# Strassen's algorithm for the fourth column block of w1 and w3 in an fp32 decoder trunk

## The chip, the core and the metric

The kernel runs on one core of a Trainium2 chip. A core has five engines that run their own instruction streams and meet at semaphores: TensorE (PE, matrix products into PSUM), VectorE (DVE), ScalarE (ACT), GpSimd (POOL) and SyncE (SP, which here only issues transfers), and 16 DMA engines that move data between HBM and the on-chip SBUF. The metric is the device time of one execution in microseconds, lower is better; the profile of one further execution shows where the time lies.

## The reference

Two layers, each of three sublayers with a layer norm behind it: an FFN, a mixer, an FFN. 256 tokens, width 1024, FFN width 2816, everything in float32.

```python
def _swiglu(x, w1, w3, w2):
    return (jax.nn.silu(x @ w1) * (x @ w3)) @ w2
...
    for l in range(DEPTH):
        h = _swiglu(x, ffn_w1[l, 0], ffn_w3[l, 0], ffn_w2[l, 0])
        x = _layernorm(ALPHA * x + 0.5 * h, ln_g[l, 0], ln_b[l, 0])
        h = _mixer(x, l, w_in[l], gate_b[l], ...)
        x = _layernorm(ALPHA * x + h, ln_g[l, 1], ln_b[l, 1])
        h = _swiglu(x, ffn_w1[l, 1], ffn_w3[l, 1], ffn_w2[l, 1])
        x = _layernorm(ALPHA * x + 0.5 * h, ln_g[l, 2], ln_b[l, 2])
```

The change concerns the four FFNs: x (256 x 1024) times w1 and w3 (1024 x 2816), silu of the first times the second, and its transpose h as the left side of the product with w2 (2816 x 1024).

## The kernel before

Every number is kept as a high part (fp32r, made by ScalarE: `A.activation(hi, src, AF.Copy)`) and a low part (what is left, made by VectorE's subtraction), and each product is three matmuls: high x high, high x low, low x high (`three`, line 259). One matmul has 128 rows of tokens (an x tile as the stationary operand) and 512 columns of weights; the contraction runs over 8 tiles of 128.

Weights come as pieces of 128 x 2048 floats (1 MB, four k-tiles of 512 columns). `fetch` (line 152) issues the transfer on SyncE's queue into one of four `raw` buffers; `stream` (line 165) splits it into two pairs of high and low tiles of 128 x 1024 out of eight `hi` and eight `lo` buffers, in steps of `sub` columns. SyncE, ScalarE and VectorE run ahead of TensorE as far as these buffers allow. A tile's buffer is free when its last reader is done; who wants it stands at the head of its queue until then.

An FFN (`ffn`, line 710) takes the first 16 and the last 4 of the 22 column tiles as five blocks of 512 columns (`NB = 5`), and the two tiles left, 16 and 17, with the weights as the stationary operand (`gemm_a2`, line 264). The first block of the first FFN goes through `gemm_first` (line 451). The others go through `gemm_b2` (line 423): four transfers (w1 and w3, each in two halves of k); first all of them for the upper 128 tokens, then all for the lower 128, so that all eight pairs of high and low tiles of the block are held until the second pass frees them. At the end of each pass `done` (line 718) applies silu on ScalarE (723), multiplies on VectorE (724) and hands the 128 x 512 result to `turned` (730). This brings it into transposed form beside the following matmuls: GpSimd parts the floats into two planes of 16-bit halves (`parted`, 196), a transposing DMA on SyncE's queue turns them (`moved`, 201), GpSimd joins them again (`joined`, 206), and h is split into high and low parts (743, 745).

The order on TensorE is the program's order. The work beside it is written as generators: `beside` (line 137) registers one, and `beat` (124), called after each group of matmuls, counts time in beats of 12 matmuls of 512 columns and resumes the generators that are due. So `wait` in `turned` is the number of beats between `parted` and the transposing DMA. The other engines' instructions are put into their queues by a scheduler that follows the program's order (`tc.cur_priority`, raised by `step` with each fetch) where buffers allow; `behind(ins)` puts an instruction behind another one on the same engine.

The product with w2 (`gemm_seven`, line 323) already uses Strassen's algorithm for the first eight k-tiles: with 2 x 2 blocks of h (two halves of tokens, two of k) and of w2, seven block products in place of eight, of sums of blocks. The sums of h are made by `sums_of_h` (752). Sums of weight blocks are made by `plus` (VectorE) or by `gather` (a transfer on GpSimd's queue that adds to what is in the buffer). Between the products the other k-tiles run (`between`, 386).

The norm behind each FFN (`Norm`, 543) loads scale and shift into the pair of `bc` buffers of the pool `res` (`bc_load`, 537). The tiles of `done` use the same `bc` buffers for odd blocks (the second and the fourth), and the `val` buffers for even ones. In the last FFN ScalarE scales the loaded row at once (559).

PSUM has eight banks of 128 x 512 floats, four with the tag `main`, four with `side`. SBUF tiles of 128 x 512 floats come from the pools `tmp` (`main`: 3, `side`: 4) and `act` (`slot`: 26).

Of the kernel before, what the change touches and what calls it, by code (L numbers as in the profile page):

```python
# [54 lines left out]
def trunk(ctx, tc, x, xT, w13a, w13b, w2, wb, wqk, wu, wg, wgr, wbr, wbrr, wo, gateb, gatebr, sgug, sgub, sguwT, sgubias, lam, diffg,  # L55
# [96 lines left out]
    def fetch(src, width=CH, raw=None):  # L152

        step()
        if raw is None:
            raw = raw_pool.tile([P, CH], F32, tag="raw", name=name("raw"))
        for g in gate:
            g[0] -= 1
        while len(gate) > 1 and gate[1][0] < 0:
            gate.pop(0)  # L160
        with behind(gate[0][1] if gate and gate[0][0] < 0 else None):
            loaded[0] = nc.sync.dma_start(raw[:, :width], src).ins
        return raw
# [32 lines left out]
    def parted(src, out):  # L196

        for w in range(2):
            G.tensor_copy(out=planes(out)[:, w], in_=numbers(src)[:, w])  # L199
# [10 lines left out]
    def transposed(src, out, via, lead, first, second, eng, to=None):  # L210

        if lead:
            yield lead
        with behind(behind_norm[0] if lead else None):
            parted(src, out)
        yield first
        with behind(loaded[0]):
            moved(out, via)  # L220
        yield second
        joined(via, out if to is None else to, eng)
# [99 lines left out]

    def gemm_seven(src, xh, xl, sums, spare, ln, done):
# [13 lines left out]
        def gather(raw, more):  # L337
            step()
            for o in range(0, CH, HC):
                G.dma_start(raw[:, o : o + HC], more[:, o : o + HC], accum_op=ALU.add)  # L340
            return raw

        def plus(raw, more):
            for o in range(0, CH, HC):
                V.tensor_tensor(out=raw[:, o : o + HC], in0=raw[:, o : o + HC], in1=more[:, o : o + HC], op=ALU.add)  # L345
            return raw

        def pieces(raw):
            out = []
            for o in range(0, CH, HC):  # L350
                hi = hi_pool.tile([P, HC], F32R, tag="hi", name=name("whi"))
                lo = lo_pool.tile([P, HC], F32R, tag="lo", name=name("wlo"))
                split(hi, lo, raw[:, o : o + HC])
                out.append((hi, lo))
            return out

        def product(ps, x, w, start, stop):
            for k in range(4):
                hi, lo = (v[:, k % 2 * 512 : k % 2 * 512 + 512] for v in w[k // 2])
                for n, (y, o) in enumerate(((hi, 0), (lo, 0), (hi, 1))):  # L360
                    PE.matmul(ps, x[o](k), y, start=start and k == n == 0, stop=stop and k == 3 and n == 2,  # L361
                              skip_group_check=True)
                beat(0.25)

# [6 lines left out]
        def rows(t, c, k0, piece, o=0, n=512):  # L371
            for j in range(2):
                k = k0 + j
                hi, lo = (w[:, j * 512 + o : j * 512 + o + n] for w in piece)
                for m, (y, x) in enumerate(((hi, xh), (lo, xh), (hi, xl))):
                    PE.matmul(q[c][t][:, :n] if o == 0 else more[:, :n], x(k)[:, t * P : (t + 1) * P], y,  # L376
                              start=k == 8 and m == 0 and (c, t) != (1, 0), stop=k == FT - 1 and m == 2, skip_group_check=True)
            beat(n / 1024)

        def block(t, k0):  # L380
            return tuple(lambda k, f=f: f(k0 + k)[:, t * P : (t + 1) * P] for f in (xh, xl))
# [161 lines left out]
    class Norm:  # L543
# [6 lines left out]
        def __init__(self, l, i, scale, eps, after, last=False):  # L550
            self.scale, self.eps, self.last, self.done, self.front = scale, eps, last, set(), i
            self.ends, self.xhi, self.xlo = [None] * NT, {}, {}
# [122 lines left out]
        def affine(self, t, h, src, xf, pieces, two=None):  # L675
            self.done.add((t, h))
            k = 0
# [32 lines left out]
    def ffn(l, f, i, norm, last=False):  # L710
        xh, xl = parts(both)
        h_hi = [act.tile([P, 512], F32R, tag="slot", name=name("hhi")) for _ in range(FT // 2)]
        h_lo = [act.tile([P, 512], F32R, tag="slot", name=name("hlo")) for _ in range(FT // 2)]
        hh, hl = view(h_hi), view(h_lo)

        def front(n, wait):

            def done(t, ps):
                pool, tag = ((act, "val"), (res, "bc"))[n % 2]
                p = pool.tile([P, D], F32, tag=tag, name=name("planes"), bufs=2).rearrange("p (w c) -> p w c", w=2)  # L720
                s = p[:, 1]
                with behind(norm.xhi[1, 0] if norm and (n, t) == (0, 0) else None):
                    silu[0] = A.activation(s, ps[0], AF.Silu).ins  # L723
                added[0] = V.tensor_tensor(out=s, in0=s, in1=ps[1], op=ALU.mult).ins  # L724
                beside(turned(n, t, s, p, wait[t]), 0)
                if norm is None and (n, t) == (1, 0):
                    beside(setup(s[:, :1]), 0)
            return done

        def turned(n, t, s, p, wait):  # L730
            lead = 3.5 if n == 0 and norm else 0
            to = slots("held", 2)[0] if n < 2 else p[:, 0]
            yield from transposed(s, p[:, 0], p[:, 1], lead, wait - lead, 0.6, G, to)
            x = to.rearrange("p (k t) -> p k t", k=4)
# [3 lines left out]
            for j in range(2) if (n, t) != (0, 1) else ():  # L738
                k = (n * 4 if n < NB - 1 else FT - 4) // 2 + j
                hi, lo = (v[k].rearrange("p (k t) -> p k t", k=2)[:, :, t * P : (t + 1) * P] for v in (h_hi, h_lo))  # L740
                f = x[:, 2 * j : 2 * j + 2]
                with behind(silu[0]):
                    A.activation(hi, f, AF.Copy)
                with behind(added[0]):
                    V.tensor_tensor(out=lo, in0=f, in1=hi.bitcast(F32), op=ALU.subtract)
# [6 lines left out]
        def sums_of_h():  # L752

            h11, h21, h12, h22 = (held[v] for v in ((0, 0), (0, 1), (1, 0), (1, 1)))
            made = [[[v[j].rearrange("p (k t) -> p k t", k=2)[:, :, P:] for j in range(2)] for v in (h_hi, h_lo)]]
            made += [[slots("sum", 2, F32R) for _ in range(2)] for _ in range(2)]
            made.append([[tmp.tile([P, 512], F32R, tag="side", name=name("sum"), bufs=4)] for _ in range(2)])
            sums[:] = [tuple(lambda k, v=v: hh_(v, k) for v in (h_hi, h_lo))]
            sums.extend(tuple(lambda k, v=v: v[0][:, k * P : (k + 1) * P] for v in m) for m in made[1:])
            for n, (out, a, b, op) in ((0, (h22, h21, h22, ALU.subtract)), (2, (h21, h11, h21, ALU.subtract)),  # L760
                                       (1, (h11, h22, h11, ALU.subtract)), (3, (h12, h12, h11, ALU.add))):
                V.tensor_tensor(out=out, in0=a, in1=b, op=op)
                w = 512 // len(made[n][0])
                for j, (hi, lo) in enumerate(zip(*made[n])):
                    f = out[:, j * w : (j + 1) * w]
                    split(hi, lo, f.rearrange("p (k t) -> p k t", k=2) if n == 0 else f)
                yield 1

        def hh_(v, k):
            return v[k // 2][:, k % 2 * T + P : k % 2 * T + T]  # L770

        for n in range(NB):
            srcs = [w13b[l, f, m * NB + n] for m in range(2)]
            if n == 0 and norm is None:
                gemm_first(srcs, front(n, (10.3, 10.3)))
            else:
                gemm_b2(srcs, xh, xl, front(n, (13.3, 10.3)), norm=norm if n == 0 else None)
        for j in range(FA, FT - 4, 2):
            for m, z in gemm_a2([w13a[l, f, j - FA + m] for m in range(2)], both, lambda m: t512("silu")):
# [3 lines left out]
                split(hh(j + m), hl(j + m), s)  # L783
# [400 lines left out]
```

## Time and profile before

| | us |
|---|---|
| median of three runs | 1199.59 (1199.42 to 1200.43) |
| the profiled execution, device time | 1198.81 |
| its span, first to last instruction | 1197.1 |
| mean granted TensorE clock | 0.999 of full speed |

| stretch of the profiled execution | us from the start |
|---|---|
| first FFN: blocks, tiles 16 and 17, w2 | 5.1 to 183.1 |
| first layer's mixer, second FFN | 183.1 to 597.4 |
| third FFN: five blocks | 597.4 to 706.2 |
| third FFN: tiles 16 and 17 | 706.2 to 717.3 |
| third FFN: w2 | 717.3 to 775.0 |
| second layer's mixer, fourth FFN, end | 775.0 to 1197.1 |

How to read it: engines run beside each other, so busy times do not add up to the span. A row of a group reads line, engine, operation, output and inputs by the program's names, shapes, count, then busy us and mean ns of one, then the idle time of the engine before them and what ended it. A row of windows gives, for a stretch in us, the busy time and instruction count of each engine, the granted clock, the share of the DMA engines and GB/s. A row of the chain of waits in order of time has start, duration and the work. A row of waits has engine, line, what was waited for, the total us, how often, the longest. A row of transfers has the queue, the count, the size and the median us from issue to landing. Matmuls are pipelined: the duration of one (about 390 ns) is longer than the spacing of two.

### The profile page before, as it was taken

The numbers are of one execution on the slowest core, as the hardware profiler recorded it, in microseconds if no ns is written. First come the engines' busy times: TensorE is split into PE (matmuls) and PEld (weight loads), VectorE is DVE, ScalarE is ACT, GpSimd is POOL, SyncE is SP. The second block draws the span as 40 slices with busy tenths as digits, with TensorE's granted clock in tenths as the row PEclk, the third lists the DMA queues.
The fourth block names the chain that finished last, engine by engine and source line by source line (L and its number), as shares of the span: only waits on it lengthen the run. The fifth ranks groups of instructions, "written<-read, shape, count | busy, mean of one in ns | idle before, by whom it ended". The sixth has DMA issues, their size and how long they took to land.

```text
span 1197.1 us, 16880 instructions
## 1 busy us (share of the span) xinstructions
PE 1191.1 (100%) x5819; PEld 1002.1 (84%) x5819; DVE 958.4 (80%) x1632; ACT 745.9 (62%) x1424; POOL 363.0 (30%) x458
## 2 busy tenths in 40 slices
PE   9999999999999999999999999999999999999998
PEld 8888888888888888888888888888888888888887
DVE  6677989797689985769886769888966989777795
ACT  7466667668855664646665656666788556564670
POOL 1425201256421233251042351004564012325310
PEclk9999999999999999999999999999999999999999
DMA  9957966767865667689676679586666764775880
GB/s 350 332 163 238 273 263 211 260 198 233 243 218 169 211 220 220 193 245 265 238 241 205 196 241 275 223 287 232 214 203 200 254 193 150 269 230 178 265 253 36
DMA packets 126310, 271.97 MB, mean 227 GB/s; under 512 B 88672, under 2 KB 89744, under 8 KB 100112
## 3 DMA queue, kind: packets, MB, share of 16 engines
q1 hardware_dynamic: 119664, 248.80, 62.4%
q0 software_dynamic: 6128, 21.57, 7.4%
q8 instruction: 45, 0.74, 0.2%
q10 hardware_dynamic: 432, 0.52, 0.1%
q14 instruction: 41, 0.34, 0.1%
HBM read 244.91 MB, written 1.05 MB: 205 GB/s over the span
## 4 chain that ended last, share of the span: by engine, by line
PE 98%; DVE 1%; DMA 1%; ACT 0%; issue 0%; ACTq 0%
PE bank L262 53%; PE bank L274 15%; PE bank L376 9%; PE bank L281 8%; PE sbank L361 5%; PE sbank L376 3%; PE bank L480 2%; PE sbank L843 1%; PE bank L361 1%; PE sbank L899 1%; PE sbank L1017 1%; DMA bc<-in_lng 0%; PE sbank L897 0%; DMA xraw<-in_xT 0%; DVE wlo L186 0%; PE sbank L644 0%
## 5 line engine op out<-in xcount | busy, mean ns | idle before, releaser
L186 DVE TENSOR_TENSOR wlo<-raw,whi 128x512 fp32r<-128x512 f32 (+1 forms) x534 | 473.2, 927 | 52.4 <-ACT whi L184 36.0
L184 ACT ACTIVATE whi<-raw 128x512 fp32r<-128x512 f32 (+1 forms) x538 | 396.1, 782 | 165.7 <-PE bank L262 92.7
L262 PE MATMUL bank<-whi,x 128*128 128x512 f32 x1480 | 460.5, 390 | 0.0
L262 PEld LDWEIGHTS bank<-whi,x 128*128 128x128 f32 x1480 | 277.8, 188 | 57.7
L262 PE MATMUL bank<-wlo,x 128*128 128x512 f32 x740 | 288.0, 389 | 0.0
L199 POOL COPY planes<-planes 128x512 uint16<-128x512 uint16 x80 | 109.6, 1398 | 240.4 <-DVE planes L724 209.4
L262 PEld LDWEIGHTS bank<-wlo,x 128*128 128x128 f32 x740 | 138.9, 188 | 28.3
L274 PE MATMUL bank<-x,whi 128*128 128x512 f32 x640 | 153.3, 391 | 0.0
L274 PEld LDWEIGHTS bank<-x,whi 128*128 128x128 f32 x640 | 118.2, 188 | 23.8
L724 DVE TENSOR_TENSOR planes<-planes,bank 128x512 f32<-128x512 f32 x40 | 27.4, 684 | 75.3 <-issue 60.7
L723 ACT ACTIVATE planes<-bank 128x512 f32<-128x512 f32 x40 | 23.9, 596 | 99.4 <-PE bank L262 97.1
L281 PEld LDWEIGHTS bank<-x,wlo 128*128 128x128 f32 x640 | 81.4, 191 | 2.9
L281 PE MATMUL bank<-x,wlo 128*128 128x256 f32 x640 | 82.6, 283 | 0.0
L228 DVE TENSOR_TENSOR wlo<-raw,whi 128x1024 fp32r<-128x1024 f32 (+1 forms) x56 | 58.5, 1071 | 26.9 <-issue 18.4
L226 ACT ACTIVATE whi<-raw 128x1024 fp32r<-128x1024 f32 (+1 forms) x56 | 52.0, 937 | 42.5 <-DVE raw L345 18.8
L376 PE MATMUL bank<-whi,hhi 128*128 128x512 f32 (+1 forms) x182 | 68.2, 374 | 0.0
L376 PE MATMUL bank<-whi,hlo 128*128 128x512 f32 (+1 forms) x182 | 67.9, 373 | 0.0
L376 PE MATMUL bank<-wlo,hhi 128*128 128x512 f32 (+1 forms) x182 | 67.9, 373 | 0.0
L686 POOL COPY nvia<-ntwo 128x256 uint16<-128x256 uint16 x20 | 9.8, 538 | 155.9 <-DMA ntwo<-nvia 138.3
L819 POOL TENSOR_TENSOR swap<-swap,sin_t 128x512 f32<-128x512 f32 x16 | 26.5, 1655 | 100.8 <-DMA swap<-z 79.5
L282 ACT ACTIVATE r<-bank 128x256 f32<-128x256 f32 x96 | 34.7, 372 | 29.4 <-PE bank L281 29.4
L208 POOL COPY planes<-planes 128x512 uint16<-128x512 uint16 x48 | 36.8, 807 | 17.8 <-DMA planes<-planes 17.4
(246 smaller groups left out, 1857.7 us busy)
## 6 DMA issues: line engine op xcount, KB each, us to landing
raw<-in_w13b SPq DMA_DIRECT2D x76, 1024.0 KB, 5.9
raw<-in_w SPq DMA_DIRECT2D x32, 1024.0 KB, 5.3
raw<-in_wb SPq DMA_DIRECT2D x16, 1024.0 KB, 6.4
raw<-in_wqk SPq DMA_DIRECT2D x16, 1024.0 KB, 6.6
raw<-in_w13a SPq DMA_DIRECT2D x8, 1024.0 KB, 5.2
spare<-in_w SPq DMA_DIRECT2D x8, 1024.0 KB, 5.9
raw<-in_wgr SPq DMA_DIRECT2D x8, 1024.0 KB, 5.4
raw<-in_wg SPq DMA_DIRECT2D x8, 1024.0 KB, 5.1
```

Of the source, the lines that this page charges most:

```text
L184: A.activation(h, r, AF.Copy)
L186: eng.tensor_tensor(out=w, in0=r, in1=h.bitcast(F32), op=ALU.subtract)
L199: G.tensor_copy(out=planes(out)[:, w], in_=numbers(src)[:, w])
L208: eng.tensor_copy(out=numbers(out)[:, w], in_=planes(src)[:, w])
L226: a = A.activation(hi, src, AF.Copy).ins
L228: return a, eng.tensor_tensor(out=lo, in0=src, in1=hi.bitcast(F32), op=ALU.subtract).ins
L262: PE.matmul(ps, xx, w, start=start and n == 0, stop=stop and n == 2)
L274: PE.matmul(b[-1], hi[:, k * P : (k + 1) * P], xc(k), start=k == 0, stop=False)
L281: PE.matmul(b[n][:, :T], lo[:, k * P : (k + 1) * P], xc(k)[:, :T], start=False, stop=k == KT - 1)
L282: emptied[0] = A.activation(r[:, s], b[n][:, T:], AF.Copy, scale=scale).ins
L361: PE.matmul(ps, x[o](k), y, start=start and k == n == 0, stop=stop and k == 3 and n == 2, skip_group_check=True)
L376: PE.matmul(q[c][t][:, :n] if o == 0 else more[:, :n], x(k)[:, t * P : (t + 1) * P], y, start=k == 8 and m == 0 and (c, t) != (1, 0), stop ...
```

## The change

The fourth block of w1 and w3 (columns 1536 to 2047) is computed by Strassen's algorithm (`seven`). One 2 x 2 matrix of blocks stands for both: the two halves of k are its rows, w1 and w3 its columns, and the two halves of the tokens and of k divide x. The seven products, 12 matmuls each, take the place of the block's 96 matmuls. They are not run together: `seven` is a generator that is resumed after certain units of the second, third and fifth blocks. Four sums of blocks of x are made and split once per FFN (`sums_of_x`); in the first FFN the blocks of x are loaded for it again from HBM on GpSimd's queue.

The second, third and fifth blocks no longer hold four transfers at once: each transfer (a unit) is split in steps of 1024 columns and used for both halves of the tokens directly, into four banks. Silu runs when the w1 half of the block is complete (`gate_`), the multiplication when the w3 half is (`done`).

The byte planes of all blocks but the first are parted by ScalarE instead of GpSimd. A tile of h now holds four k-tiles of one token half, so that its split is one instruction of 512 columns instead of two of 256. The tiles of `done` take `bc` buffers in the second and the fifth block. The beats until the transposing DMA are shorter. `rows` and `block` in `gemm_seven` call `x(k, t)` instead of slicing; `gather`, `plus`, `pieces` and `product` move out of it unchanged but for `halved`, which lets a piece be a pair of 1024-column tiles.

```diff
@@ fetch
+            if isinstance(raw, list):
+                for j, v in enumerate(raw):
+                    loaded[0] = nc.sync.dma_start(v, src[:, j * HC : (j + 1) * HC]).ins
+            else:
+                loaded[0] = nc.sync.dma_start(raw[:, :width], src).ins
@@ parted
+            o, i = planes(out)[:, w], numbers(src)[:, w]
+            if by is A:
+                A.activation(o, i, AF.Copy)
+            else:
+                G.tensor_copy(out=o, in_=i)
...
+    def gather(raw, more):
+        step()
+        for j, v in enumerate(halved(raw)):
+            G.dma_start(v, more[:, j * HC : (j + 1) * HC], accum_op=ALU.add)
+        return raw
+
+    def plus(raw, more):
+        for v, m in zip(halved(raw), halved(more)):
+            V.tensor_tensor(out=v, in0=v, in1=m, op=ALU.add)
+        return raw
...
@@ ffn
+            def gate_(t, ps):
+                pool, tag = ((act, "val"), (res, "bc"))[n in (1, NB - 1)]
...
+                    silu[0] = A.activation(p[:, 1], ps, AF.Silu).ins
+
             def done(t, ps):
...
+                added[0] = V.tensor_tensor(out=s, in0=s, in1=ps, op=ALU.mult).ins
+                beside(turned(n, t, s, p[:, 0], wait[t]), 0)
...
+            yield from transposed(s, p, s, lead, wait - lead, 0.6, G, to, A if n else G)
...
+            if (n, t) != (0, 1):
+                split(h_hi[2 * n + t], h_lo[2 * n + t], to, after=(silu[0], added[0]))
...
+        def sums_of_x():
+
+            if norm is None:
+                t11, t12 = (s512("xsum") for _ in range(2))
+                t21, t22 = (t512("xsum") for _ in range(2))
+                for v, t, h in ((t21, 1, 0), (t22, 1, 1), (t11, 0, 0), (t12, 0, 1)):
+                    G.dma_start(v.rearrange("p (k t) -> p k t", k=4),
+                                xT.rearrange("p (k t) -> p k t", t=T)[:, 4 * h : 4 * h + 4, t * P : (t + 1) * P])
+                yield 4
+            else:
+                t11, t12, t21, t22 = (norm.rows[v] for v in ((0, 0), (0, 1), (1, 0), (1, 1)))
...
+            made = [[home(v) for v in w] for w in (("main", "side"), ("side", "main"), ("main", "slot"), ("side", "slot"))]
+            yield from strassen_sums(x_sums, made, t11, t21, t12, t22)
+
+        def strassen_sums(to, made, v11, v21, v12, v22):
...
                 V.tensor_tensor(out=out, in0=a, in1=b, op=op)
+                if n in (2, 3):
+                    yield 1
+            for n, out in ((0, v22), (2, v21), (1, v11), (3, v12)):
+                split(*made[n], out)
                 yield 1
...
+        def seven(src, x_sums):
...
+            bx, bz, bq = (side_bank() for _ in range(3))
+            g0, v0, v1, g1 = (slots("seven", 2)[0] for _ in range(4))
+            r1 = fetch(w11)
+            product(bx, x11, pieces(r1), True, False)
+            A.activation(g0, bx, AF.Copy)
+            yield
+            product(bq, x12, pieces(fetch(w21)), True, True)
+            V.tensor_tensor(out=g0, in0=bq, in1=g0, op=ALU.add)
+            A.activation(g0, g0, AF.Silu)
+            r2 = fetch(w12, raw=[hi_pool.tile([P, HC], F32, tag="hi", name=name("r2")) for _ in range(2)])
+            yield
+            product(bz, x_sums[0], pieces(plus(r1, r2)), True, False)
+            A.activation(v1, bz, AF.Copy)
+            gather(r2, w22)
+            r3 = fetch(w22, raw=[lo_pool.tile([P, HC], F32, tag="lo", name=name("r3")) for _ in range(2)])
+            yield
+            product(bx, x_sums[1], pieces(plus(r1, r3)), False, False)
+            A.activation(v0, bx, AF.Copy)
+            gather(r1, w21)
+            yield
+            product(bz, x_sums[3], pieces(r3), False, True)
+            V.tensor_tensor(out=v0, in0=bz, in1=v0, op=ALU.subtract)
+            V.tensor_tensor(out=g0, in0=g0, in1=v0, op=ALU.mult)
+            beside(turned(3, 0, g0, v0, 8.3), 0)
+            yield
+            product(bx, x_sums[2], pieces(r2), False, False)
+            V.tensor_tensor(out=v1, in0=v1, in1=bx, op=ALU.subtract)
+            yield
+            product(bx, x22, pieces(r1), False, True)
+            A.activation(g1, bx, AF.Silu)
+            V.tensor_tensor(out=g1, in0=g1, in1=v1, op=ALU.mult)
+            beside(turned(3, 1, g1, v1, 6.3), 0)
+            yield
...
+            beside(sums_of_x(), 1)
...
+            beside(sums_of_x(), 5)
+        products, unit = seven(w13(3), x_sums), 0
+        for n in (1, 2, NB - 1):
+            ps = [[bank() for _ in range(2)] for _ in range(NT)]
+            ready = front(n, (9.3, 8.3))
+            for c in range(2):
+                for m in range(2):
+                    got = stream(w13(n)[m][:, c * CH : (c + 1) * CH])
+                    for t in range(NT):
+                        for j, piece in enumerate(got):
+                            rows_b(ps[t][m], t, 4 * c + 2 * j, piece, xh, xl, KT)
+                        if c:
+                            ready[m](t, ps[t][m])
+                    unit += 1
+                    if unit in (1, 2, 4, 6, 8, 9, 10):
+                        next(products)
```

139 lines of the change are left out of this document (66 added, 73 removed).

## The prediction

> **What bounds the kernel now.** First the head of the page and its chain of waits, then the chain in order of time, then the waits of TensorE alone.
>
> ```profile
> span 1197.1 us, 16880 instructions
> PE 1191.1 (100%) x5819; PEld 1002.1 (84%) x5819; DVE 958.4 (80%) x1632; ACT 745.9 (62%) x1424; POOL 363.0 (30%) x458
> ...
> PE 98%; DVE 1%; DMA 1%; ACT 0%; issue 0%; ACTq 0%
> ```
> ```profile
> 157.99 2.89 PE sbank L361 x12
> ...
> 597.38 108.85 PE bank L262 x480
> 706.23 7.25 PE bank L274 x32
> 713.48 3.83 PE bank L281 x32
> 717.31 2.75 PE sbank L361 x12
> 720.06 2.72 PE bank L376 x12
> ...
> 749.98 2.79 PE sbank L361 x12
> ```
> ```profile
> PE sbank L492 <- DVE warm L488: 1.1, 1, 1.1
> PE sbank L623 <- ACT minus L621: 0.7, 1, 0.7
> PE bank L480 <- ACT whi L226: 0.3, 1, 0.3
> ```
> The reader sees that 98% of the chain is TensorE's own work, that in the third FFN the 480 matmuls of all five blocks run as one piece without a hole, and that TensorE waits 2.1 us in the whole kernel, never inside the blocks that are changed. So a matmul taken away is worth its spacing, 108.85/480 = 0.2268 us, as long as its operands still arrive in time; VectorE, at 80%, is the next engine.
>
> The stages say more than the share of the whole span. Four blocks of the third FFN (the second to the fifth), the stretch in which its w2 product already runs seven block products, and the end of the kernel:
>
> ```profile
> core 0: us, PE busy (x) PEld busy (x) DVE busy (x) ACT busy (x) POOL busy (x), PEclk, DMA share, GB/s
> ...
> 619.20:706.20 87.00, 87.00 (x385) 72.03 (x385) 63.21 (x89) 44.96 (x81) 34.11 (x34) 1.00 0.70 222
> ...
> 717.30:755.50 38.20, 38.20 (x170) 31.49 (x169) 37.26 (x47) 25.71 (x34) 4.62 (x6) 1.00 0.95 294
> ...
> 1168.00:1197.00 29.00, 24.64 (x144) 20.89 (x142) 16.02 (x36) 1.46 (x4) 1.02 (x2) 0.97 0.10 37
> ```
> In the second of these rows VectorE is busy 37.26 of 38.20 us, the DMA engines 95%, and TensorE still has no hole: that is how far the other engines can be loaded when the buffers between them stay full.
>
> **The matmuls removed.** A block takes 2 row halves x 2 matrices x 8 k-tiles x 3 = 96 matmuls of 512 columns; seven products take 7 x 4 x 3 = 84. That is 12 per FFN, 48 in all, 48 x 0.2268 = 10.9 us. The four blocks then need 87.0 - 2.7 = 84.3 us per FFN.
>
> Of the price of one matmul the Trainium skill ("TensorE: Matmul & The Clock Gate", section "Back-to-back issue gap") says about 131 ns for a stream of weight loads and matmuls of 512 columns, and 216 ns for an isolated gap. By the first the 48 would be worth 6.3 us, by the second 10.4; the piece of 480 above runs at neither, and the measurement decides.
>
> **What VectorE, ScalarE, GpSimd and the DMAs get instead.** The durations, in the four blocks of the third FFN and then over the kernel:
>
> ```profile
> L186 DVE TENSOR_TENSOR wlo<-raw,whi 128x512 fp32r<-128x512 f32 x54 | 37.6, 744 | 4.2 <-ACT whi L184 3.6
> L184 ACT ACTIVATE whi<-raw 128x512 fp32r<-128x512 f32 x50 | 28.2, 622 | 11.6 <-PE bank L262 11.1 <-ACT whi L184 0.5
> L199 POOL COPY planes<-planes 128x512 uint16<-128x512 uint16 x18 | 27.3, 1546 | 49.1 <-DVE planes L724 49.1
> ...
> L724 DVE TENSOR_TENSOR planes<-planes,bank 128x512 f32<-128x512 f32 x8 | 5.5, 685 | 17.8 <-issue 15.1 <-PE bank L262 2.7
> ...
> L723 ACT ACTIVATE planes<-bank 128x512 f32<-128x512 f32 x8 | 4.8, 596 | 25.9 <-PE bank L262 25.7 <-issue 0.3
> ...
> L762 DVE TENSOR_TENSOR held<-held,held 128x512 f32<-128x512 f32 x4 | 3.0, 758 | 0.0
> ...
> L228 DVE TENSOR_TENSOR sum<-held,sum 128x512 fp32r<-128x512 f32 x3 | 2.0, 683 | 0.0
> L226 ACT ACTIVATE sum<-held 128x512 fp32r<-128x512 f32 x3 | 1.9, 628 | 0.1
> ```
> ```profile
> L228 DVE TENSOR_TENSOR wlo<-raw,whi 128x1024 fp32r<-128x1024 f32 x40 | 48.2, 1223 | 25.2 <-issue 18.4 <-ACT whi L226 6.4
> L226 ACT ACTIVATE whi<-raw 128x1024 fp32r<-128x1024 f32 x40 | 42.4, 1061 | 40.2 <-DVE raw L345 18.8 <-DMA raw<-in_w 11.4 <-PE bank L274 6.0
> ...
> L345 DVE TENSOR_TENSOR raw<-raw,spare 128x1024 f32<-128x1024 f32 x16 | 19.0, 1221 | 0.0
> ...
> L340 POOL DMA_DIRECT2D spare<-in_w x8 | 7.5, 946 | 5.8 <-DVE raw L345 4.6 <-DVE bc L539 1.2
> ...
> L637 ACT ACTIVATE nvia<-xtok 128x512 uint16<-128x512 uint16 x10 | 6.3, 628 | 3.1 <-DVE xtok L598 3.1
> ```
> VectorE, per FFN. The low parts of the weights: 64 of 512 columns before (47.6 us at 744 ns), after it 24 + 14 = 38 of 1024 (46.5 us at 1223 ns). The 744 holds copies slowed beside GpSimd; at the 683 ns of the smoother row the 64 would be 43.7, so I count +2. The two sums of weights formed here: 4 x 1.22 = 4.9. The four sums of x: 4 x (0.758 + 0.683) = 5.8. Five block results instead of two products with silu: 3 x 0.685 = 2.1. Together +14.8, so 63.2 + 14.8 = 78 of 84.3 us, 93%. The joined splits of h (one of 512 for two of 256) can only lower that; I give them nothing.
>
> ScalarE. Weights 64 x 0.622 = 39.8 become 38 x 1.061 = 40.3; sums of x 4 x 0.628 = 2.5; three copies out of PSUM 1.8; the byte-plane copies of eight tiles, which GpSimd did at 1.546 us, 16 x 0.628 = 10.0. Together +14.8: 60 of 84.3 us, 71%. GpSimd loses 16 x 1.546 = 24.7 us and gains four accumulating transfers at 0.95 us.
>
> DMA. The block's 4 MB become 6 (the second pieces are fetched again to be accumulated): 222 GB/s x 87 us = 19.3 MB, plus 2, in 84.3 us is 253 GB/s, under the 294 of the row above. The first FFN also loads 1 MB of xT on GpSimd's queue.
>
> All of this lies beside TensorE's 84.3 us, and every engine stays below what the w2 stretch carried without a hole. So I cost it at nothing; without that cover VectorE's 14.8 us would fall on the path four times, 59 us.
>
> **Waits that the change adds.** A unit (one transfer of 2048 columns, 24 matmuls) takes TensorE 5.4 us, a product 2.72. The sums of x are begun 5 beats (12 matmuls each) into the second block and the first is split 2 beats later, 19 us in; it is read by the third product, 5.4 + 2.7 + 5.4 + 2.7 + 10.9 = 27 us in. The accumulated weights have three or more units between issue and use. The banks of a block are emptied (0.596 and 0.685 us) a whole unit before the next block writes them. These are hidden.
>
> The tight place is the transfer queue. One buffer of four is held by the first piece from product 1 to 7, and the next two pieces are loaded into two high and two low buffers, so that SyncE stands before them until TensorE has freed these, with all later weights behind. Units 1 and 2 and products 1 and 2 fill the eight high buffers, so the next to come free are unit 1's.
>
> ```profile
> SPq L162 <- DVE wlo L186: 520.2, 119, 14.4
> ```
> ```profile
> raw<-in_w13b SPq DMA_DIRECT2D x76, 1024.0 KB, 5.9
> ...
> spare<-in_w POOLq DMA_DIRECT2D x8, 512.0 KB, 10.2
> raw<-in_w POOLq DMA_DIRECT2D x8, 512.0 KB, 7.3
> ```
> SyncE already spends 520 us standing before buffers, so standing is normal. Freed by unit 1 at 5.4 us, the buffers let the third piece go, and unit 3's transfer behind it: 1 MB at 294 GB/s (3.6 us) + 5.9 to land + 1.06 + 1.22 for its first split = 11.8 us, and TensorE wants it 2.72 + 5.44 + 2.72 = 10.9 us later. So the stall is between nothing (the first of the two buffers is free 1.4 us sooner) and 0.9 us per FFN. I take 0.2, near the 0.17 that the longest product of the w2 stretch shows above its 2.72 (the row at 157.99); 0.8 us in all.
>
> **The sum.** Made on the profiled execution, 1198.81 us (its span and 1.7 us around it): 1198.81 - 10.9 + 0.8 = 1188.7. The median of the runs lies 0.78 above it, so 1189.5.
>
> **The rivals.**
>
> *Weights late.* The stall above takes its full 0.9 us, in each FFN once or at the low buffers too: +2.8 to +6.4, so 1192.3 to 1195.9. For it: the landing time and the two split times of the rows leave no reserve in 10.9 us. Against: SyncE starts the first half of the third piece 1.4 us sooner, and before the block's end VectorE is already splitting for the next one.
>
> *The norm's load late.* The fifth block's tiles now sit in the pair of buffers that the following norm's scale and shift need; before, the fourth block's did, one block sooner. In the last FFN ScalarE waits for that load:
>
> ```profile
> 1136.06 0.58 POOL L540 DMA_DIRECT2D bc<-in_lng  x1 [7.01 <-DMA spare<-in_w]
> ...
> 1141.03 1.06 ACT L559 ACTIVATE bc<-bc 128x1024 f32<-128x1024 f32 x1 [1.43 <-DMA bc<-in_lng]
> ```
> It can cost at most the 4.97 us from issue to that instruction, once, where it cost 1.43: +3.5, 1193.0.
>
> *Slower: VectorE stands before PSUM.* Its instructions run in order, and a read of a bank that stands ahead of a split holds all later splits.
>
> ```profile
> DVE planes L724 <- issue: 60.7, 12, 6.7
> ```
> These waits now cost nothing, for all pieces of the block have been split by then. With units split one by one, the reads of banks (six by the blocks' products, three by the sums over products 2, 5 and 6) stand among splits of the next units. If three of the nine hold it, at the mean of that row, 60.7/12 = 5.1 us, they take 15.2 us; VectorE has 84.3 - 78 = 6.3 free, so 8.9 us fall on TensorE, less the 2.7 gained: +6.2 per FFN, 1224. It decides from 9.0 us of such waiting per FFN (6.3 + 2.7). Against it: in the w2 stretch the folds stand likewise among splits, with 0.9 us free and no hole.
>
> Only the window at the end shows holes, and there the granted clock is 0.97. The Trainium skill (the same TensorE page, "Part 1: The HAM clock gate") has the clock halve after an idle window of about 3.4 us; by that rule stalls in one piece would each cost some more, and many short ones nothing.
>
> **Chances.** What a measurement can tell from no change is 0.2%, 2.4 us: faster is below 1197.2, slower above 1202.0. Forecast, 1188.3 to 1191: 0.57. Weights late: 0.16. Norm late: 0.06. VectorE in part, its waits nearly eating the gain (1197 to 1202): 0.06. VectorE in full: 0.15. So faster 0.79, same 0.06, slower 0.15. The range runs from 1188.0 (no stall, and the spread of the runs) to 1197.0, which holds all but the last two cases.
>
> **What would show it.** Right: 5771 matmuls instead of 5819; the second to fifth blocks of each FFN 84.3 to 84.6 us with granted clock 1.00; the seven products as pieces of 2.72 to 2.9 us between units of 5.4. Weights late: TensorE waiting for a high or low part before unit 3 or 5, released by a transfer. Norm late: a hole of some us once, in the last FFN's w2 stretch, behind line 559's instruction. VectorE: idle before the reads of the product banks and TensorE holes behind them. The forecast is wrong if the four blocks take over 86 us anywhere.

## The result, and the profile after

| | before | after |
|---|---|---|
| median of the runs | 1199.84 us (1199.42 to 1200.43) | 1213.8 us (1211.48 to 1215.57) |
| ratio to before | | 1.0115, 95% interval 1.0092 to 1.0137 |
| profiled execution, its span | 1198.81, 1197.1 us | 1212.16, 1210.1 us |

The change makes the kernel 1.15% slower; 0.8% faster (1189.5 us) was forecast. The head of the page of the kernel after, its chain of waits by engine, and the longest waits of TensorE (what was waited for, the sum, how often, the longest):

```profile
span 1210.1 us, 16672 instructions
PE 1187.0 (98%) x5771; PEld 993.5 (82%) x5771; DVE 1033.7 (85%) x1548; ACT 798.6 (66%) x1372; POOL 333.2 (28%) x414
...
PE 84%; DVE 9%; DMA 5%; issue 2%; ACT 1%; SPq 0%; DVEq 0%; ACTq 0%
```
```profile
PE sbank L358 <- DVE wlo L236: 8.5, 5, 2.6
PE bank L270 <- DVE wlo L190: 5.6, 5, 3.3
```
The 48 matmuls are gone (5771), yet TensorE's share of the chain has fallen from 98% to 84%, and VectorE and transfers fill the rest: low parts of weights that come too late. Where, the stages tell. The windows of the third FFN's four blocks and of its w2 product in the kernel after (stretch, then busy us and count of each engine, granted clock, share of the DMA engines, GB/s):

```profile
629.20:714.20 85.00, 84.51 (x373) 69.70 (x372) 76.92 (x76) 56.39 (x73) 25.64 (x21) 1.00 0.84 241
725.40:784.70 59.30, 57.17 (x253) 46.75 (x253) 53.81 (x74) 35.74 (x50) 9.51 (x10) 1.00 0.82 262
```
and the w2 product of the kernel before:

```profile
717.30:774.00 56.70, 56.70 (x254) 46.78 (x253) 52.23 (x77) 35.75 (x53) 5.24 (x7) 1.00 0.82 264
```
The four blocks hold half a microsecond without a matmul, the w2 product, whose arithmetic the change doesn't touch, 2.1. For the whole kernel I measured each stage in the traces from its first matmul to the first of the next stage (the w2 products over the first 252 of TensorE's matmuls and transposes, which leaves out the last 4, in the last FFN the last 42), and added up the four FFNs: how much longer the first blocks are than before (87.24 us), the four blocks than four times the 84.3 of the prediction (four times 84.32, or 337.28), and the w2 products than before (223.53). For the change: first blocks +1.6, four blocks +9.1 (89.29, 86.55, 85.10, 85.43), w2 products +12.0 (58.96, 61.29, 59.39, 55.91 against 56.89, 56.73, 56.79, 53.12). That is 22.7 of the 23.9 us between 10.9 saved and 13.0 lost in the span; the rest lies between these stages.

**The w2 product.** SyncE and GpSimd around the start of the third FFN's w2 product, in order of time, first before (it starts at 717.15), then after (725.35):

```profile
703.55 8.12 SPq L203 DMA_TRANSPOSE planes<-planes  x2
...
713.27 1.45 POOL L208 COPY planes<-planes 128x512 uint16<-128x512 uint16 x2 [1.39 <-DMA planes<-planes]
716.86 0.82 SPq L162 DMA_DIRECT2D spare<-in_w  x2
```
```profile
725.06 0.82 SPq L166 DMA_DIRECT2D spare<-in_w  x2
725.97 7.37 SPq L211 DMA_TRANSPOSE planes<-planes  x2
...
734.62 2.56 POOL L216 COPY planes<-planes 128x512 uint16<-128x512 uint16 x2 [1.00 <-ACT whi L188]
734.81 3.38 DVE L190 TENSOR_TENSOR wlo<-raw,whi 128x1024 fp32r<-128x1024 f32 x2
738.02 2.46 POOL L216 COPY planes<-planes 128x512 uint16<-128x512 uint16 x2 [0.84 <-DMA planes<-planes]
738.12 3.37 DVE L342 TENSOR_TENSOR raw<-raw,spare 128x1024 f32<-128x1024 f32 x2
...
743.94 0.50 PE L358 MATMUL sbank<-wlo,sum 128*128 128x512 f32 x1 [1.86 <-DVE wlo L236]
```
The order on SyncE has turned round. The transposes of the fifth block hang on the last transfer issued (`behind(loaded[0])`), and since they are issued a beat or two sooner, that transfer is now a `spare` one; issued later, they hang on a piece of w2 that stands ahead of the spare transfers on the queue. Those two stand until the x buffers come free at the end of `gemm_a2`, so the transposes, whose first was issued 13.3 us ahead of them before, now come 0.9 us behind. Reckoned from the start of the w2 product, GpSimd's last joins begin 12.7 us after it instead of 3.9 ahead, and the splits of h behind them fall into the stretch in which VectorE has least time; each pair of VectorE's instructions beside a join takes 3.4 us instead of 2.36 (the same pair, undisturbed, elsewhere in this trace), and product 4 waits 1.86 us.

In the second FFN, the worst of the four (+4.6 us), the same wait is 2.64 us, and the granted clock drops behind it. A window of that stretch, in the kernel after:

```profile
566.00:568.00 2.00, 2.00 (x6) 1.62 (x5) 2.00 (x4) 2.00 (x3) 0.78 (x2) 0.50 0.76 176
```
The eleven matmuls of product 4 behind the wait take 4.2 us instead of 2.5, so some 1.7 of the 4.6 us are the clock's. It does not drop behind every wait: behind the 1.86 us of the third FFN and the 3.3 us that TensorE waits in the first FFN's blocks it is 1.00.

**The four blocks.** In the third FFN of the kernel after: SyncE's load of w22, the second term of product 4's sum of two weights, and that sum on VectorE; then VectorE around product 6:

```profile
647.95 1.07 SPq L164 DMA_DIRECT2D r<-in_w13b  x2
...
657.85 1.23 DVE L342 TENSOR_TENSOR raw<-raw,r 128x1024 f32<-128x1024 f32 x1 [5.70 <-DMA r<-in_w13b]
```
```profile
688.51 0.76 DVE L809 TENSOR_TENSOR held<-held,held 128x512 f32<-128x512 f32 x1
689.20 1.20 DVE L843 TENSOR_TENSOR seven<-seven,seven 128x512 f32<-128x512 f32 x1
690.32 1.19 DVE L809 TENSOR_TENSOR held<-held,held 128x512 f32<-128x512 f32 x1
691.43 1.19 DVE L236 TENSOR_TENSOR hlo<-held,hhi 128x512 fp32r<-128x512 f32 x1
692.55 0.68 DVE L809 TENSOR_TENSOR held<-held,held 128x512 f32<-128x512 f32 x1
693.16 1.21 DVE L190 TENSOR_TENSOR wlo<-raw,whi 128x1024 fp32r<-128x1024 f32 x1
694.29 0.68 DVE L809 TENSOR_TENSOR held<-held,held 128x512 f32<-128x512 f32 x1
694.89 1.73 DVE L190 TENSOR_TENSOR wlo<-raw,whi 128x1024 fp32r<-128x1024 f32 x1
```
VectorE stands 5.70 us before this transfer, with unit 6's splits behind it in its order; from there it works to the end of the blocks almost without a pause. By the program the transfer is the plain load of the fourth piece into two low buffers (`r3`), not an accumulating one, as two of the expectations below have it. Later the four sums of h (line 809), which came as late before (56 us into the four blocks, now 59), fall among the splits of units 9 and 10 and the results of product 5, some of them beside GpSimd's joins (0.68 becomes 1.20, 1.21 becomes 1.73). Whether the wait or the burst decides, the trace alone doesn't say. This FFN shows the pattern, but lost only 0.8 of the 9.1 us; the first lost 5.0, with a wait of 2.5 us at the same place and another 5.1 us in which VectorE waits for high parts from ScalarE.

### The profile page after: what moved, and what is told of

Read it like the earlier page. It is cut to its first block, busy times and chain, and to the rows that moved or that the text cites. A ratio compares the mean times of both kernels' runs of the same rounds, so it can differ in the third digit from the quotient of the medians.

```text
span 1210.1 us, 16672 instructions
## 1 busy us (share of the span) xinstructions
PE 1187.0 (98%) x5771; PEld 993.5 (82%) x5771; DVE 1033.7 (85%) x1548; ACT 798.6 (66%) x1372; POOL 333.2 (28%) x414
## 3 DMA queue, kind: packets, MB, share of 16 engines
HBM read 254.35 MB, written 1.05 MB: 211 GB/s over the span
## 4 chain that ended last, share of the span: by engine, by line
PE 84%; DVE 9%; DMA 5%; issue 2%; ACT 1%; SPq 0%; DVEq 0%; ACTq 0%
PE bank L270 42%; PE bank L282 15%; PE bank L289 7%; PE sbank L358 7%; PE bank L387 5%; PE sbank L387 3%; DVE wlo L190 2%; DMA spare<-in_w 2%; DVE wlo L236 2%; DVE raw L342 2%; DMA raw<-in_w 1%; PE bank L491 1%; DVE held L809 1%; PE sbank L945 1%; DVE hlo L236 1%
## 5 line engine op out<-in xcount | busy, mean ns | idle before, releaser
L190 DVE TENSOR_TENSOR wlo<-raw,whi 128x1024 fp32r<-128x1024 f32 (+1 forms) x374 | 428.2, 1176 | 43.0 <-ACT whi L188 30.3
L188 ACT ACTIVATE whi<-raw 128x1024 fp32r<-128x1024 f32 (+1 forms) x378 | 351.4, 959 | 148.3 <-PE bank L270 39.4
L270 PE MATMUL bank<-whi,x 128*128 128x512 f32 x1224 | 386.3, 390 | 0.0
L270 PEld LDWEIGHTS bank<-whi,x 128*128 128x128 f32 x1224 | 229.8, 188 | 47.5
L270 PE MATMUL bank<-wlo,x 128*128 128x512 f32 x612 | 239.0, 391 | 5.7 <-DVE wlo L190 5.6
L270 PEld LDWEIGHTS bank<-wlo,x 128*128 128x128 f32 x612 | 114.9, 188 | 31.7 <-DVE wlo L190 8.6
L236 DVE TENSOR_TENSOR wlo<-raw,whi 128x1024 fp32r<-128x1024 f32 (+1 forms) x96 | 113.9, 1205 | 18.1 <-ACT whi L234 7.5
L234 ACT ACTIVATE whi<-raw 128x1024 fp32r<-128x1024 f32 (+1 forms) x96 | 92.9, 982 | 38.3 <-DVE raw L342 18.6
L216 POOL COPY planes<-planes 128x512 uint16<-128x512 uint16 x32 | 40.7, 1329 | 55.2 <-DMA planes<-planes 30.4
L205 ACT ACTIVATE planes<-planes 128x512 uint16<-128x512 uint16 x48 | 27.4, 619 | 31.0 <-DVE planes L751 31.0
L216 POOL COPY held<-planes 128x512 uint16<-128x512 uint16 x32 | 46.2, 1645 | 5.6 <-DMA planes<-planes 5.6
L216 POOL COPY seven<-seven 128x512 uint16<-128x512 uint16 x16 | 20.9, 1353 | 77.4 <-DMA seven<-seven 38.2
```

Of the source, the lines that this page charges most:

```text
L188: A.activation(h, r, AF.Copy)
L190: eng.tensor_tensor(out=w, in0=r, in1=h.bitcast(F32), op=ALU.subtract)
L216: eng.tensor_copy(out=numbers(out)[:, w], in_=planes(src)[:, w])
L234: a = A.activation(hi, src, AF.Copy).ins
L236: return a, eng.tensor_tensor(out=lo, in0=src, in1=hi.bitcast(F32), op=ALU.subtract).ins
L270: PE.matmul(ps, xx, w, start=start and n == 0, stop=stop and n == 2)
```

## The experiments

Each kernel is the change with the edits shown. "Stages" gives the three sums as above, over the same bases: first blocks, four blocks, w2 products; for the change +1.6, +9.1, +12.0. Three accounts stand against each other: single instructions and transfers stand at the wrong place in the order of a queue; VectorE has too much to do as a whole; or weights one transfer at a time are too tight. The kernel before was run beside each group: 1199.94, 1200.11, 1199.8 and 1200.05 us.

**Transposes ahead again (e1).**
```
-            ready = front(n, (9.3, 8.3))
+            ready = front(n, (10.3, 9.3) if n == NB - 1 else (9.3, 8.3))
```


> Edit: the fifth block's transposing DMAs are due one beat later, so that they stand on SyncE's queue before the two transfers into the spare buffers instead of behind them. Theory A (the holes of the w2 stretches come from these transposes: they wait behind the spare transfers, which wait for the x buffers, and GpSimd's joining copies then fall on VectorE's fullest part): the four w2 stretches go from 59.9, 62.2, 60.3 and 69.4 us back to the 57.8, 57.7, 57.7 and 65.5 of before, the time from 1213.8 to about 1201. Theory B (VectorE's added work is the bound and the place of the holes is accidental): the holes move, the time stays within 3 us of 1213.8.

1204.91 us (1202.27 to 1207.78), ratio 1.0045 (1.0029 to 1.0061). Stages +1.7, +10.2, +4.1. The third FFN's blocks and w2 product:

```profile
621.58:707.61 86.03, 84.90 (x373) 69.70 (x372) 76.96 (x77) 56.40 (x74) 24.92 (x21) 1.00 0.89 237
718.70:775.42 56.72, 56.72 (x254) 46.98 (x253) 51.71 (x74) 35.44 (x50) 4.53 (x6) 1.00 0.81 264
```
The w2 product is whole again with one beat's difference, in three FFNs; what is left of its +4.1 lies in the last one (57.27 against 53.12). The holes in the blocks stay (+10.2), so they have another cause.

**The fourth block plain (e2).**
```
-            beside(sums_of_x(), 1)
-            beside(sums_of_x(), 5)
-        products, unit = seven(w13(3), x_sums), 0
-        for n in (1, 2, NB - 1):
+        for n in range(1, NB):
...
-                    if unit in (1, 2, 4, 6, 8, 9, 10):
-                        next(products)
```


> Edit: Strassen undone, the rest of the change kept: the fourth block is a plain block of 96 matmuls, read one transfer at a time like its neighbours, no sums of x; the done tiles alternate their buffers as before. Theory A: the four blocks take 87.1 us without a hole, the w2 stretches keep their holes (13 us in all), the time is about 1213. Theory B: without Strassen's 18 us of VectorE work per FFN nearly all holes go, 1200 to 1202. Theory C (one transfer at a time leaves too short a lead): the blocks themselves take more than 88 us.

1260.17 us (1257.85 to 1260.78), ratio 1.05. Stages +0.3, the four blocks exactly as before (87.04 in each FFN), w2 products +60.4. That one transfer at a time is by itself too tight falls: it costs nothing. The size of the loss was missed by far: 1213 us was the highest time named. Here the transposes stand behind the spare transfers too, and the chain of waits of the third FFN leads through them:

```profile
750.62 19.93 DMA planes<-planes
770.55 0.05 issue
770.60 1.42 POOL planes L216 x2
772.02 6.80 issue
```
So this order of the transfers arises without Strassen's algorithm for the fourth block, and with it the w2 products are 15.0 to 17.4 us longer in three FFNs. No run turns the order back in this kernel, so that it accounts for all of the loss is not shown, nor why the transposes land so late. In the third FFN TensorE waits 11.4 us for high parts of weights, whose splits stand behind those of h on ScalarE; behind the longest of these waits the clock is low (0.69 from 765 to 780 us, 0.81 from 780 to 800). The mean granted clock of this run was 0.976; 0.999 in the change.

**Sums of h later (e3).**
```
             if (n, t) == (1, 1):
-                yield 1
+                yield 6
                 yield from sums_of_h()
```


> Edit: the sums of h begin 5 beats (13.6 us) later. Theory A: the burst on VectorE around products 5 and 6 and units 9 and 10 is spread, the holes there (0.5 to 3.5 us per FFN) go, the four blocks take together 3 to 6 us less, time 1208 to 1211. Theory B: no change, since the same work is done.

1205.34 us (1202.02 to 1206.65), ratio 1.0042 (1.0026 to 1.0057). Stages +2.5, +1.2, +13.2. The third FFN's blocks:

```profile
626.46:710.78 84.32, 84.32 (x374) 69.87 (x372) 76.71 (x77) 56.39 (x73) 35.77 (x20) 1.00 0.89 259
```
VectorE does the same work there as in the change (76.71 against 76.92 us) and TensorE has no hole: that VectorE has too much to do falls for the blocks. These are the 84.3 us of the prediction.

**Sum of weights behind the splits (e12).**
```
-            product(bx, x_sums[1], pieces(plus(r1, r3)), False, False)
+            product(bx, x_sums[1], pieces(plus(r1, r3, low[0])), False, False)
```
where `plus` issues its additions behind the last subtraction so far (`low[0]`, unit 6's).

> The change with one edit alone: product 4's sum of weights behind unit 6's last subtraction on VectorE. If VectorE's wait for the accumulated transfer is a cause of its own in the blocks: the four blocks 0.5 to 1 us shorter per FFN (85.1 to 86.5 become 84.6 to 85.8), w2's stretches as in the change; 1210 to 1212 us. If the h sums' burst is the only cause there: blocks unchanged, 1213 to 1215 us.

1205.71 us (1204.47 to 1212.78), ratio 1.0061 (1.0037 to 1.0085). Stages +2.1, +2.4, +10.7: the blocks nearly whole (84.35, 85.14, 85.13, 85.06), more than I expected. So the wait and the burst are not two losses that add; the holes need both, and taking away either mends most.

**Joins on ScalarE (e11).** All blocks but the first: line 216's copies by `A.activation(..., AF.Copy)`.

> The change with one edit alone: the joining copies on ScalarE for all blocks but the first, everything else where the change has it, the fifth block's transposes behind the spare transfers still. If GpSimd's copies beside VectorE are the cause of the holes in w2's stretch: three stretches of 57 to 58 us instead of 59 to 61, VectorE busy 20 us less, 1202 to 1207 us. If the place of the transposes is the cause and the slowing only adds to it: the stretches still 58.5 to 61, 1207 to 1213 us.

1205.84 us (1203.41 to 1209.62), ratio 1.0043 (1.0027 to 1.0058). The profiled execution took 1209.62 us: stages +2.1, +7.0, +11.4. VectorE's busy time falls from 1033.7 to 1004.3 us, 29.4 us for 64 copies of GpSimd fewer, 0.46 us each. The holes of the w2 product stay (59.72, 60.91, 58.48, 55.84), as the place of the transposes would have it; the median is in the range given to the slowing. So both seem to have a part, and how much the slowing is worth by itself stays open. The Trainium skill ("SBUF — State Buffer", section "Who interferes with whom") says that a VectorE instruction with both inputs in SBUF and a GpSimd instruction that reads SBUF exclude each other, whichever starts later waiting. The trace agrees as far as it goes: VectorE's instructions of this kind take some 0.5 us more beside a copy.

**xT later (e4).** The four loads of xT in the first FFN, `with behind(...)` GpSimd's last parting copy of the first block.

> Edit: in the first FFN the four loads of xT stand on GpSimd's queue behind the parting copies of the first block instead of starting at 1.4 us. Theory A: the first block ends at 27.2 us as before instead of 28.8, the rest is as in the changed kernel, about 1212.2. If the 1.6 us are the spread of the weights' own transfers: no change.

1212.96 us (1210.51 to 1216.01), ratio 1.0111. Stages +0.1, +10.2, +11.6: the first block is as before (21.90 us for 23.39), and the same FFN's blocks lose it again (92.17 for 89.29), for VectorE now stands before the loads:

```profile
42.27 0.69 DVE L810 TENSOR_TENSOR xsum<-xsum,xsum 128x512 f32<-128x512 f32 x1 [9.23 <-DMA xsum<-in_xT]
```

**Together (e5, e6).** e5 has the edits of e1 and e3, and the last norm's scaling by -0.5 twelve beats later; e6 has e12's as well.

> The change with three things moved and nothing taken out: the sums of h five beats later, the fifth block's transposes one beat later (ahead of the spare transfers), the norm's negated scale 12 beats later in the last FFN. Theory A (what went wrong is where single instructions and transfers stand, each place by itself): the two gains add up. Four blocks 84.3 to 85.2 us in every FFN, w2's stretches 56.7 to 56.9 in three FFNs and 53.2 to 54.5 in the last, the first block of the first FFN still 1.5 to 2.5 us longer than before; 1190 to 1194 us. Theory B (VectorE's work as a whole is too much, and what is pushed out of one place comes up in another): w2's stretch keeps 2 us or more of holes per FFN; 1197 to 1202 us.

> As the run before, and product 4's sum of two weights stands behind unit 6's last subtraction on VectorE instead of ahead of it, so that waiting for the accumulated transfer no longer holds a split. If that wait still reaches TensorE: the four blocks 0.3 to 1 us shorter per FFN, 1 to 3 us in all. If the sums of h coming later have already taken the tightness away: within 0.6 us of the run before in the median, blocks unchanged at 84.3 to 84.6.

e5: 1199.5 us (1195.9 to 1201.16), ratio 0.9991 (0.998 to 1.0001); the profiled execution took 1195.9 us, stages +2.1, +0.8, +4.0. e6: 1195.69 (1194.39 to 1197.41), ratio 0.9966 (0.9953 to 0.9979), the profiled execution 1196.21 us, stages +2.2, 0.0, +5.2. e5's median lies in the range that I had given to too much work on VectorE, though its holes are not spread over all FFNs as that account would have it. The gains add only in part: e1 and e3 give back 8.9 and 8.5 us, e5 with both edits and a third 14.3. By the medians e12's edit is worth 3.8 us even after e3's, where I had given it 3 at most; the profiled executions differ by 0.3 us the other way, so no trace shows where the 3.8 lie. In e6 all four FFNs take 84.32 us for the blocks:

```profile
616.68:701.00 84.32, 84.32 (x374) 69.82 (x372) 76.19 (x77) 56.89 (x74) 35.48 (x20) 1.00 0.88 260
```

**Parting by GpSimd (e7), joins on ScalarE (e8), both on e6.**

> As e6, but the eight x tiles are parted into byte planes by GpSimd again, 16 copies of some 1.5 us per FFN, as in the kernel before. If VectorE and GpSimd slow each other: VectorE's subtractions of 1024 columns beside these copies take 1.6 to 1.8 us instead of 1.2, VectorE has no time left in the four blocks (78 us of 84.3 plus 16 x 0.5), and they come to 86 to 90 us: 1196 to 1212 us. If they don't (the slowing seen beside GpSimd's copies is something else): within 1 us of e6, since GpSimd has the time.

> As e6, but the joining copies of the transposed planes go to ScalarE too (16 of some 0.63 us per FFN), for all blocks but the first, so that GpSimd copies nothing beside the blocks. If VectorE and GpSimd slow each other: VectorE's busy time in the whole kernel falls by 10 us or more, and the holes that are left shrink; time the same as e6 or up to 3 us less. If ScalarE's 70 us of 84.3 is then the tight engine: high parts late, blocks over 85 us, 1 to 6 us more than e6.

e7: 1223.05 us (1221.14 to 1228.06), ratio 1.0188 (1.0171 to 1.0205). Slower, but not as I expected: VectorE's subtractions did not lengthen (1290 ns, 1307 in e6) and three FFNs keep 84.32 us for the blocks. The loss comes in the first FFN's blocks (94.13), in `gemm_a2` (8.2 us in all) and in the w2 products (+18.5). The second FFN of e7:

```profile
522.59 3.13 POOL L207 COPY seven<-seven 128x512 uint16<-128x512 uint16 x2
...
525.74 1.24 SPq L211 DMA_TRANSPOSE seven<-seven  x1
527.08 1.00 SPq L166 DMA_DIRECT2D raw<-in_w13a  x2
...
532.64 1.06 ACT L188 ACTIVATE whi<-raw 128x1024 fp32r<-128x1024 f32 x1 [7.87 <-DMA raw<-in_w13a]
```
GpSimd's late parting holds the transpose, the transpose holds SyncE's queue, and behind it come the weights of `gemm_a2`. The move of the parting to ScalarE, which the change made, is worth 27 us in this order of things.

e8: 1194.1 us (1193.07 to 1196.33), ratio 0.9955 (0.994 to 0.9969), the lowest median of the kernels that compute the whole. VectorE's busy time falls by 22 us, ScalarE carries 64.83 of 84.32 us in the blocks without a hole. Stages +1.4, 0.0, +3.4; of the w2 products' part, 3.1 in the last FFN, where ScalarE stands before the norm's load:

```profile
1138.27 1.06 ACT L577 ACTIVATE bc<-bc 128x1024 f32<-128x1024 f32 x1 [5.42 <-DMA bc<-in_lng]
1139.23 1.99 ACT L238 ACTIVATE whi<-raw 128x1024 fp32r<-128x1024 f32 x2
```

**What is left (e9, e10, e13, e14, all on e8).** In e9 and e10 the scaling by -0.5 comes behind the last use of the scale, so the last norm is computed with the scale as it was loaded. In e10 the loads of xT stand `behind` a matmul, in e14 VectorE first writes a column of each buffer from the last x tile of the block. In e13 and e14 GpSimd does the scaling.

> As e8, and the norm's negated scale ten beats later still in the last FFN, since in e8 ScalarE stood 5.42 us before it for the load of the norm's scale, with the high part of the next w2 weights behind. If that wait is what is left there: the last FFN's w2 stretch 53.2 to 54.2 us instead of 56.2, the rest unchanged; 1191 to 1192.5 us. If the stretch is long because the load itself delays w2's transfers: 55 us or more, 1193.5 to 1194.5.

> As e9, and the first FFN's four loads of xT behind the matmuls of the fifth and sixth k-tile of the first block (some 18 us in) instead of at the very start, with the sums of x two beats later. If the early loads take transfer time from the first weights: the first block 21.8 to 22.2 us instead of 23.1, the first FFN's other blocks still 84.3 to 84.6; 1189.5 to 1191.5 us. If the loads are late now for the sums, as in e4: the first FFN's blocks 86 us or more and 1192 or more.

> As e8, but GpSimd instead of ScalarE multiplies the norm's scale by -0.5 in the last FFN, so that the wait for its load stands on GpSimd's queue, where only two gathers follow, and no split of w2's weights stands behind it. If that wait (5.42 us of ScalarE in e8) is what makes the last w2 stretch long: 53.2 to 54.3 us instead of 56.2, 1191 to 1192.5 us. If the transfers themselves are late there: 55 us or more and 1193.5 to 1194.5.

> As e13, and the four loads of xT start only when the first block's last x tile is split (some 15 us in), by a column that VectorE writes into each buffer first; the sums of x two beats later. If the early loads (and the sums that VectorE then makes in the midst of the first block) are what makes the first block long: 21.8 to 22.2 us instead of 23.1 to 24.7, the first FFN's other blocks 84.3 to 84.6, 1189 to 1191 us. If the sums now come too late, as in e4: blocks over 86 us, 1192 to 1198 us.

With no wait for the load, e9's last w2 product takes 53.63 us, within 0.5 of before. But e10's, with the same edit, takes 55.01 and e13's 54.57, with short holes elsewhere: without the wait 1.2 to 2.6 of the 3.1 us go. The medians (1195.85, 1193.29 and 1195.6 us) show no gain over e8's that is clear of the spread. e10's loads still started at 1.36 us, so it says nothing of xT. In e14 they start 17.85 us in, and it loses: 1198.83 us, first block 25.53, the blocks of that FFN 87.65:

```profile
26.90 0.69 DVE L819 TENSOR_TENSOR xsum<-xsum,xsum 128x512 f32<-128x512 f32 x1 [6.78 <-DMA xsum<-in_xT]
```
The sum stands on VectorE ahead of the second block's first splits, as in e4. Where these loads would cost nothing was not found.

## Why the prediction was wrong

- **The matmuls removed: right.** 5771 matmuls; four blocks of 84.32 us in every FFN of e6, 10.9 us saved.
- **The loads of the engines: right, but not what decides.** Forecast for the four blocks were 78 us of VectorE, 60 of ScalarE and 253 GB/s; the third FFN of the change has 76.9, 56.4 and 241 in 85.0 us. e3 has the same loads and no hole.
- **The step that failed** is "All of this lies beside TensorE's 84.3 us, and every engine stays below what the w2 stretch carried without a hole. So I cost it at nothing". A sum of busy times says that there is room in the stretch, not that each instruction finds it before it is needed. VectorE has 7.4 us free in the third FFN, and its wait ahead of product 4's sum, with splits behind it, is 5.7 us there (2.5, 4.7 and 4.6 in the others). With the burst of the sums of h this costs 9.1 us, of which e3 gives back 7.9, e12 6.7 and e6 all. Why the first FFN, with the shortest wait, loses most stays open.
- **Left out:** the transposes' place on SyncE. The text costs every instruction that is added, and the beats until the transposes are shorter, as the section on the change says, but it never asks which transfer they then stand behind. That is the larger part of the +12.0 us in the w2 products; e1 gives back 7.9 of it.
- **The wrong cover:** the sums of h, the same in number, were not looked at again, although the splits of other units now stand around them; and the w2 stretch, quoted as the proof of how full VectorE can be (37.26 of 38.20 us), was also the place with only 0.9 us in reserve for what arrived late in it.
- **Weights late, 0.2 us per FFN at the third piece: not seen.** TensorE does not wait at product 3, and in e6 nowhere in the four blocks, so the 0.8 us were too many. It was the fourth piece, at the low buffers which the rival names, that came late, and the first to suffer was VectorE's order, not TensorE.
- **VectorE stands before PSUM, 1224 us: right in kind.** An instruction waiting ahead of splits did matter; what it waited for was the load of the fourth piece instead of a bank (before banks VectorE waits 1.5 us in the third FFN's blocks, not 15.2), and it cost 9.1 us in all, with the sums of h, where that rival had 8.9 per FFN.
- **Norm's load late, +3.5: right in kind,** beside the other losses instead of in their place. The last w2 product is 4.2 us longer than before in e1 and 3.1 in e8; taking the wait away gives back 1.2 to 2.6 of the latter.
- **The clock behind stalls: named, but without a term in the sum.** One wait in the change brought it down, for some 1.7 us, while others of like length did not.

The forecast time, 1189.5 us, was not reached: e8 is 4.6 us above it, 1.4 of them in the first blocks, 3.4 in the w2 products by its profile.

## What to carry to other kernels

Free time on an engine covers added work only in the order in which its queue stands: for each instruction that is moved or given a new wait, write down what is next behind it on its queue and when that is due. An instruction tied to "the last transfer issued" changes its place when anything in front of it moves, so look for such ties in the diff, not only for the instructions that it adds. When a stretch shows an engine at 97%, it proves that the engine can work so, and also that little more may arrive there.

## What the runs showed that was not expected

- One copy of GpSimd costs VectorE 0.46 us on the average of 64 copies between the change and e11 (29.4 us), 0.35 between e6 and e8 (1026.0 to 1003.9 us) and 0.21 between e6 and e7 (1026.0 to 1039.7), so it depends on what runs beside it. The copy itself lengthens too: the joins into `planes` take 1329 ns in the change, 807 before.
- Losses do not add like terms of a sum. In the medians e1, e3, e11 and e12 each give back 8 to 9 us of the change, 33.4 together, while e8 with all four edits (and a fifth) gives back 19.7, and no more than 24.3 lay between the change and the forecast.
